# Second expert product turned round, features by tokens, and 160 instead of 128 tokens served by gathered rows

## The chip, the cores and the metric

The kernel runs on one core of a Trainium2 chip. The metric is the device time of one execution in microseconds. Engines are named as the profile names them: PE multiplies matrices (PEld is its weight load), DVE and ACT work on vectors, POOL does vector work and issues the indirect DMAs, SP issues most other DMAs.

## The reference

One encoder layer over 512 tokens of 1,024 features: two sequence mixers side by side (a state-space scan and a chunked scan), merged, then a layer of 16,384 experts, of which each token uses 128 (8 heads, 16 each), and a last norm. All is 32-bit. Only the expert layer is touched by the change:

```python
expert = (i1 * PEER_NKEYS + i2).reshape(t, PEER_HEADS * PEER_TOPK)     # 128 of 16384 for each token
gates = jax.nn.softmax(best_s, axis=-1).reshape(t, PEER_HEADS * PEER_TOPK)
...
hid = jnp.einsum('td,tkd->tk', xb, u_tab[eb])
act = jax.nn.gelu(hid, approximate=False) * gb
return jnp.einsum('tk,tkd->td', act, v_tab[eb])
```

## The kernel before

The four tiles of 128 tokens are served in two ways.

Tile 0 is **gathered** (`gathered`, L1082): for each of its 128 picks an indirect DMA on POOL fetches one row of the table per token (`rowg`, 512 KB, four buffers, three fetched ahead), 128 times from `u` and 128 times from `v`. DVE multiplies a row of `u` with the token and sums it (L1103), and adds a row of `v`, scaled, to `acc0` (L1113).

Tiles 1 to 3 are **dense** (`dense`, L1027): all 16,384 experts for all 384 tokens, in 128 blocks of 128 experts. For a block `up` (L1034) loads a tile of the transposed `u` (`w_raw`, 512 KB), splits it into a high and a low part (`wload` L137: ACT casts to `w_hi` at L143, POOL or DVE subtracts to `w_lo` at L144), and runs 24 matmuls (`mm3`, L151 to L153: 8 feature blocks, three products of parts) into `hid` [128 experts, 384 tokens]; ACT applies gelu into `F`. The second product then loads the block's rows of `v` (`v_raw`, 512 KB, three buffers of its own), splits them (`vh`, `vl`, L156 and L157), multiplies `F` with the gates (L1062), splits that (`Wh`, `Wl`), and runs 18 matmuls (L1074 to L1076) with 128 tokens as the stationary side and 512 features as the moving side, into six accumulators [128 tokens, 512 features] that stay in PSUM for all blocks.

`w_raw` has three buffers, `w_hi` and `w_lo` two each. All loads of `w_raw`, `v_raw` and the gates `G8` (1.5 MB for 8 blocks, two buffers) stand in SP's one queue, in a fixed order, each waiting for its buffer.

The gates come from `route_pick` (L921, DVE) and `gates` (L976): for each tile of tokens eight steps of 16 tokens, in which DVE, ACT and POOL build one-hot matrices, PE multiplies them (L1020), ACT copies the result (L1021) and SP stores it to DRAM (`G_d`, L1024). The first 34 `up` (NF = 34) run ahead of the dense loop and fill PE during this stage. `G8` is read back from `G_d` once all of it is stored. At the end `finish` (L1117) adds, norms and stores the four tiles.

A scheduler sets each engine's fixed order from the program's order and its own estimates; each engine then takes its list in order. The dense loop with the gathered steps between its blocks is this:

```python
for i, _ in enumerate(self.dense()):
    owed += GATHER if i < 128 - NF else (256.0 - GATHER * (128 - NF)) / (NF - 4)
    while owed >= 1.0:
        next(gathered, None)
        owed -= 1.0
```

## Time and profile before

| | |
|---|---|
| three runs | 1957.99, 1961.28, 1967.22 us (median 1961.28) |
| span of the profiled execution | 1962.9 us (no time of its own is given beside the span) |
| front and merge | to about 592 us |
| routing scores | 592 to 755 us |
| picks and gates, with `up` as filling | 755 to 1004 us |
| rest of the 34 `up` | 1004 to 1028 us |
| dense loop with both products | 1028 to 1814 us |
| dense loop, second product alone | 1814 to 1954 us |
| final norm and stores | 1954 to 1963 us |

The profiled execution lies between the middle and the slowest of the three runs, 1.6 us above the median. In the slices of the page each digit is the busy share of a fortieth of the span (49 us) in tenths.

### The profile page before, as it was taken

How to read it: one execution, taken by the hardware profiler on the slowest of the kernel's cores; microseconds unless marked ns; L12 is line 12 of the kernel's file. 1: busy time of each engine (PE TensorE's matmuls, PEld its weight loads, DVE VectorE, ACT ScalarE, POOL GpSimd, SP SyncE). 2: the span in 40 equal slices, each digit the busy share in tenths (PEclk: the TensorE clock that was granted, in tenths of full speed). 3: DMA queues.
4: the chain of work that ended last, by engine and by line, in shares of the span. 5: the costliest groups of instructions: out<-in, count | busy, mean ns of one | idle time of the engine just before them, and what ended most of it. 6: DMA issues, size and time to landing. Idle time of an engine off the chain costs nothing.

```text
span 1962.9 us, 27293 instructions
## 1 busy us (share of the span) xinstructions
PE 1817.9 (93%) x9447; PEld 1580.4 (81%) x9447; DVE 1498.9 (76%) x3238; ACT 836.4 (43%) x1426; POOL 774.4 (39%) x637
## 2 busy tenths in 40 slices
PE   6778889999998987887899999999999999999998
PEld 4666667767887877877898999999999999999886
DVE  7999875677645789998867977777777777777676
ACT  4333545455332333967762333333333333333333
POOL 3364403444112345554543543343434343343341
PEclk9889899999999998998999999999999999999999
DMA  4212153454552223424379998889899889886665
GB/s 141 91 44 82 54 139 125 157 155 141 199 180 79 98 80 129 183 108 183 119 250 334 363 334 294 305 309 313 278 314 313 301 283 313 306 284 230 234 259 200
DMA packets 174826, 407.45 MB, mean 208 GB/s; under 512 B 20000, under 2 KB 77088, under 8 KB 171616
## 3 DMA queue, kind: packets, MB, share of 16 engines
q1 hardware_dynamic: 129472, 258.27, 39.0%
q0 software_dynamic: 36864, 134.23, 19.3%
q10 hardware_dynamic: 8352, 13.21, 1.9%
q8 instruction: 74, 1.21, 0.3%
q14 instruction: 64, 0.52, 0.1%
HBM read 367.28 MB, written 37.32 MB: 206 GB/s over the span
## 4 chain that ended last, share of the span: by engine, by line
PE 59%; DVE 10%; ACT 2%; DMA 2%; issue 1%; POOL 1%; DVEq 0%; POOLq 0%; ACTq 0%
PE acc L1075 9%; PE acc L1076 9%; PE acc L1074 8%; PE hid L153 7%; PE hid L151 7%; PE hid L152 7%; PE mm L151 3%; PE mm L153 3%; PE mm L152 3%; PE sm L1020 2%; DVE oh L1001 2%; DMA G<-G_d 2%; DVE oh L1002 1%; DVE ohm L935 1%; ACT stg L1021 1%
## 5 line engine op out<-in xcount | busy, mean ns | idle before, releaser
L143 ACT CAST w_hi<-w_raw 128x1024 fp32r<-128x1024 f32 (+2 forms) x209 | 211.8, 1014 | 459.7 <-PE hid L152 220.4
L153 PE MATMUL hid<-x2h,w_lo 128*128 128x384 f32 x1024 | 357.3, 349 | 12.8 <-POOL w_lo L144 9.2
L151 PE MATMUL hid<-x2h,w_hi 128*128 128x384 f32 x1024 | 355.5, 347 | 9.7 <-ACT w_hi L143 9.7
L144 POOL TENSOR_TENSOR w_lo<-w_raw,w_hi 128x1024 fp32r<-128x1024 f32 (+1 forms) x94 | 218.6, 2327 | 361.5 <-ACT w_hi L143 354.7
L152 PE MATMUL hid<-x2l,w_hi 128*128 128x384 f32 x1024 | 355.0, 347 | 0.0
L1091 POOL DMA_INDIRECT rowg<-in_u_dram,idx x128 | 191.8, 1498 | 276.8 <-DVE rowg L1103 191.9
L1076 PE MATMUL acc<-vh,Wl 128*128 128x512 f32 x768 | 300.7, 392 | 0.0
L1075 PE MATMUL acc<-vl,Wh 128*128 128x512 f32 x768 | 300.6, 391 | 0.0
L1074 PE MATMUL acc<-vh,Wh 128*128 128x512 f32 x768 | 298.5, 389 | 0.0
L1091 POOL DMA_INDIRECT rowg<-in_v_dram,idx x128 | 167.6, 1310 | 272.2 <-DVE acc L1113 209.1
L144 DVE TENSOR_TENSOR w_lo<-w_raw,w_hi 128x1024 fp32r<-128x1024 f32 (+1 forms) x115 | 140.9, 1225 | 169.1 <-ACT w_hi L143 169.1
L153 PEld LDWEIGHTS hid<-x2h,w_lo 128*128 128x128 f32 x1024 | 197.6, 193 | 14.8 <-POOL w_lo L144 11.0
L151 PEld LDWEIGHTS hid<-x2h,w_hi 128*128 128x128 f32 x1024 | 197.4, 193 | 14.2 <-ACT w_hi L143 10.5
L156 ACT CAST Wh<-F 128x384 fp32r<-128x384 f32 x128 | 65.9, 515 | 317.8 <-PE acc L1075 279.7
L152 PEld LDWEIGHTS hid<-x2l,w_hi 128*128 128x128 f32 x1024 | 197.3, 193 | 3.7
L1076 PEld LDWEIGHTS acc<-vh,Wl 128*128 128x128 f32 x768 | 144.1, 188 | 30.3
L157 DVE TENSOR_TENSOR vl<-v_raw,vh 128x1024 fp32r<-128x1024 f32 x128 | 156.2, 1220 | 14.2 <-ACT vh L156 13.3
L1075 PEld LDWEIGHTS acc<-vl,Wh 128*128 128x128 f32 x768 | 144.1, 188 | 28.5 <-DVE vl L157 0.2
L1074 PEld LDWEIGHTS acc<-vh,Wh 128*128 128x128 f32 x768 | 144.2, 188 | 28.3 <-ACT vh L156 0.4
L1113 DVE SCALAR_TENSOR_TENSOR acc<-rowg,act,acc 128x1024 f32<-128x1024 f32 x127 | 162.4, 1279 | 5.9 <-DMA rowg<-in_v_dram,idx 5.7
L1103 DVE SCALAR_TENSOR_TENSOR rowg<-rowg,xn 128x1024 f32<-128x1024 f32 x128 | 152.0, 1219 | 5.1 <-DMA rowg<-in_u_dram,idx 5.1
L153 PE MATMUL mm<-xh,w_lo 128*128 128x512 f32 (+1 forms) x328 | 136.8, 418 | 15.9 <-DVE w_lo L144 12.3
(392 smaller groups left out, 3553.1 us busy)
## 6 DMA issues: line engine op xcount, KB each, us to landing
w_raw<-in_ut_dram SPq DMA_DIRECT2D x128, 512.0 KB, 4.7
v_raw<-in_v_dram SPq DMA_DIRECT2D x128, 512.0 KB, 6.5
G_d<-stg SPq DMA_DIRECT2D x24, 1024.0 KB, 3.9
G<-G_d SPq DMA_DIRECT2D x16, 1536.0 KB, 13.8
w_raw<-in_w_in_dram SPq DMA_DIRECT2D x40, 512.0 KB, 3.6
RB<-rows_d SPq DMA_DIRECT2D x32, 256.0 KB, 5.6
w_raw<-in_w_q_dram SPq DMA_DIRECT2D x16, 512.0 KB, 3.5
E<-rows_d SPq DMA_DIRECT2D x32, 128.0 KB, 5.0
```

The lines of the kernel that those rows point to most:

```text
L143: nc.scalar.copy(hi, raw)
L144: (lo_eng or nc.vector).tensor_sub(lo, raw, hi.bitcast(F32))
L151: mm(ps, ahi(k), bhi(k), start=start and k == 0, stop=False)
L152: mm(ps, ahi(k), blo(k), start=False, stop=False)
L153: mm(ps, alo(k), bhi(k), start=False, stop=stop and k == nk - 1)
L157: (lo_eng or self.nc.vector).tensor_sub(lo, src, hi.bitcast(F32))
L1074: mm(a, wh[:, ts], vh[:, hs], start=k == 0, stop=False)
L1075: mm(a, wh[:, ts], vl[:, hs], start=False, stop=False)
L1076: mm(a, wl[:, ts], vh[:, hs], start=False, stop=k == 127)
L1091: nc.gpsimd.indirect_dma_start(out=r, out_offset=None, in_=tab, in_offset=bass.IndirectOffsetOnAxis(ap=self.idx0[:, k:k + 1], axis=0))
L1103: d = V.scalar_tensor_tensor(r, r, 1.0, self.xn0, op0=OP.mult, op1=OP.mult, accum_out=hid[:, k:k + 1])
L1113: d = V.scalar_tensor_tensor(self.acc0, r, act[:, k:k + 1], self.acc0, op0=OP.mult, op1=OP.add)
```

## The change

- **Second product**: the host hands over `v` a second time, cut as `vt[a, d]` = 8 blocks of 128 experts (a group, `a` of 16) by 128 features (`d` of 8). `down(a, d)` loads one such tile through `wload`, so through the same `w_raw`, `w_hi` and `w_lo` buffers as `up`, and runs 24 matmuls with the features as the stationary side and the tokens as the moving side. Four of the eight feature blocks stay in PSUM, the other four are added to `yT` in SBUF by DVE after each group. `Wh` and `Wl` get 12 buffers each, since a group needs eight at once.
- **Tokens**: the dense part takes the last 352 tokens (ND). The first 32 tokens of tile 1 (NX) are gathered too: 32 tokens by 4 quarters of their picks fill 128 partitions, so 32 more rows of `u` and 32 of `v` (320 gathers in place of 256). `gates` leaves out the first two steps of tile 1.
- **Pace**: NF is 28 and GATHER 2.9. The end works in five groups of rows, with transposes of `yT` for the dense ones.

```diff
-NF = 34
+NF = 28
+NX = 32
+ND = 384 - NX
-GATHER = 2.4
+GATHER = 2.9
-LAST = 2
...
     def gates(self, t):
-        slow(0)
-        for tb in range(8):
+        first = NX // 16 if t == 1 else 0
+        slow(2 * first)
+        for tb in range(first, 8):
...
     def dense(self):
-            ps = self.phid.tile([128, 384], F32, name="hid", bufs=2)
+            ps = self.phid.tile([128, 512], F32, name="hid", bufs=2)[:, :ND]
...
-            v = vp.tile([128, 1024], F32, name="v_raw", bufs=3)
-            nc.sync.dma_start(v, I["v"][i * 128:(i + 1) * 128, :])
...
-            vh = vp.tile([128, 1024], F32R, name="vh", bufs=2)
-            vl = vp.tile([128, 1024], F32R, name="vl", bufs=2)
-            self.split(vh, vl, v)
...
-            wh = vp.tile([128, 384], F32R, name="Wh", bufs=2)
-            wl = vp.tile([128, 384], F32R, name="Wl", bufs=2)
...
-                        for hf in range(2):
-                            hs = slice(hf * 512, (hf + 1) * 512)
-                            a = self.acc[2 * t + hf]
-                            mm(a, wh[:, ts], vh[:, hs], start=k == 0, stop=False)
-                            mm(a, wh[:, ts], vl[:, hs], start=False, stop=False)
-                            mm(a, wl[:, ts], vh[:, hs], start=False, stop=k == 127)
+        def weigh(i):
+            f = F.pop(i)
+            V.tensor_mul(f, f, g8[i // 8].rearrange("p b (i t) -> p b i t", t=16)[:, :, i % 8, :])
+            w = [vp.tile([128, ND], F32R, name=n, bufs=12) for n in ("Wh", "Wl")]
+            self.split(*w, f.rearrange("p b t -> p (b t)"))
+            W[i] = w
+
+        def down(a, d):
+            hi, lo = self.wload(I["vt"][a, d], 8, 128)
+            ps = held[d] if d < 4 else pacc.tile([128, 512], F32, name="dn", bufs=2)[:, :ND]
+            one = d >= 4
+            for b in range(8):
+                wh, wl = W[8 * a + b]
+                mm(ps, hi[:, b, :], wh, start=b == 0 and (one or a == 0), stop=False)
+                mm(ps, hi[:, b, :], wl, start=False, stop=False)
+                mm(ps, lo[:, b, :], wh, start=False, stop=b == 7 and (one or a == 15))
+            if a == 15 and not one or a == 0 and one:
+                A.copy(self.yT[:, d, :], ps)
+            elif one:
+                V.tensor_add(self.yT[:, d, :], self.yT[:, d, :], ps)
+
+        gate(0)
+        for b in range(8):
+            weigh(b)
+        for a in range(16):
+            if a < 15:
+                gate(a + 1)
+            for d in range(8):
+                down(a, d)
+                if NF + 8 * a + d < 128:
+                    up(NF + 8 * a + d)
+                if a < 15:
+                    for b in range(d - 4, d - 3) if d < 7 else range(3, 8):
+                        if b >= 0:
+                            weigh(8 * a + 8 + b)
+                yield
```

How the scheduler places this, at three places that the prediction speaks of. Line numbers in the rows of the change are the changed kernel's (L1082 to L1084 are `down`, L152 to L154 `mm3`, L141 the load in `wload`, L1067 the load of `G8`, L145 its subtraction to `w_lo`).

SP's queue of before, from the last stores of the gates to the second load of `G8` (printed as `G_` with a number):

```order
L140 DMA w_raw<-in_ut_dram 128x1024
L1053 DMA v_raw<-in_v_dram 128x1024
L140 DMA w_raw<-in_ut_dram 128x1024
L1056 DMA G_10273<-G_d 128x24x128
L140 DMA w_raw<-in_ut_dram 128x1024
L1053 DMA v_raw<-in_v_dram 128x1024
L140 DMA w_raw<-in_ut_dram 128x1024
L1053 DMA v_raw<-in_v_dram 128x1024
L140 DMA w_raw<-in_ut_dram 128x1024
L1053 DMA v_raw<-in_v_dram 128x1024 x2
L140 DMA w_raw<-in_ut_dram 128x1024
L1056 DMA G_10836<-G_d 128x24x128
```

The same place of the change:

```order
L1035 DMA G_d<-stg 128x2048
L141 DMA w_raw<-in_vt_dram 128x1024
L1067 DMA G_9892<-G_d 128x22x128
L1067 DMA G_9934<-G_d 128x22x128
L141 DMA w_raw<-in_ut_dram 128x1024
L1067 DMA G_10573<-G_d 128x22x128
L141 DMA w_raw<-in_vt_dram 128x1024
L141 DMA w_raw<-in_ut_dram 128x1024
L141 DMA w_raw<-in_vt_dram 128x1024
L141 DMA w_raw<-in_ut_dram 128x1024
L1067 DMA G_11196<-G_d 128x22x128
```

Three loads of `G8` now stand ahead of the third tile of `vt`, and every tile of either product takes one of the three `w_raw` buffers.

PE of before, where the first second product begins (it stands behind 816 matmuls into `hid`, 34 `up`):

```order
L151 MATMUL hid<-x2h,w_hi 128x384
L152 MATMUL hid<-x2l,w_hi 128x384
L153 MATMUL hid<-x2h,w_lo 128x384
L1074 MATMUL acc_10265<-vh,Wh 128x512
L1075 MATMUL acc_10265<-vl,Wh 128x512
L1076 MATMUL acc_10265<-vh,Wl 128x512
L1074 MATMUL acc_10266<-vh,Wh 128x512
```

PE of the change at the same place, behind 696 matmuls into `hid` (29 `up`):

```order
L153 MATMUL hid<-x2l,w_hi 128x352
L154 MATMUL hid<-x2h,w_lo 128x352
L1082 MATMUL acc_9887<-Wh,w_hi 128x352
L1082 MATMUL acc_9888<-Wh,w_hi 128x352
L1083 MATMUL acc_9887<-Wl,w_hi 128x352
L1084 MATMUL acc_9887<-Wh,w_lo 128x352
```

In both lists the last one-hot product of the gates stands behind 668 and 667 matmuls into `hid`: between it and the first second product lay 148 of them, and now 29.

PE of the change at the border of the sixth and the seventh group (numbers tell the buffers apart: `w_hi_13632` is a tile of `up`, `w_hi_13701` the next group's first of `down`, `w_hi_13731` the `up` after it):

```order
L154 MATMUL hid_13636<-x2h_5170,w_lo_13633 128x352
L1082 MATMUL acc0_9887<-Wh_13427,w_hi_13701 128x352 [waits Activation_49]
L1083 MATMUL acc0_9887<-Wl_13428,w_hi_13701 128x352
L152 MATMUL hid_13735<-x2h_5170,w_hi_13731 128x352 [waits Activation_49]
L153 MATMUL hid_13735<-x2l_5171,w_hi_13731 128x352
L1084 MATMUL acc0_9887<-Wh_13427,w_lo_13702 128x352 [waits DVE_49]
```

Here two matmuls of the next `up` stand ahead of the third matmul of `down`; it is so at 5 of the 12 borders at which `up` still runs beside `down`, and at the others the 24 matmuls of a tile stand together.

## Rows read from the trace of the kernel before

**Rows 1.** Page: the span, and the rate of the DMAs in 40 slices.
```profile
span 1962.9 us, 27293 instructions
...
GB/s 141 91 44 82 54 139 125 157 155 141 199 180 79 98 80 129 183 108 183 119 250 334 363 334 294 305 309 313 278 314 313 301 283 313 306 284 230 234 259 200
```

**Rows 2.** Windows: stretch, its length, busy us (count) of each engine, PEclk, DMA share, GB/s.
```profile
755.00:1004.00 249.00, 206.89 (x1287) 197.16 (x1286) 229.15 (x802) 184.66 (x345) 137.99 (x121) 0.90 0.40 151
1080.00:1814.00 734.00, 734.00 (x3714) 668.38 (x3714) 551.39 (x689) 257.19 (x360) 292.99 (x216) 1.00 0.88 303
1814.00:1954.00 140.00, 139.97 (x619) 115.55 (x617) 95.59 (x123) 51.69 (x78) 44.01 (x28) 1.00 0.64 233
...
1100.00:1140.00 40.00, 40.00 (x202) 36.11 (x201) 35.78 (x39) 14.67 (x20) 17.06 (x14) 1.00 1.04 388
```

**Rows 3.** Timeline of PE: start, us. The first and last of 15, then of 24.
```profile
1499.99 0.39 PE L1074 MATMUL acc<-vh,Wh 128*128 128x512 f32 x1
...
1503.41 0.33 PE L151 MATMUL hid<-x2h,w_hi 128*128 128x384 f32 x1
...
1507.60 0.39 PE L1074 MATMUL acc<-vh,Wh 128*128 128x512 f32 x1
```

**Rows 4.** Groups by form, 1080 to 1814 us: count, busy us, mean ns, idle before, releaser.
```profile
L1113 DVE SCALAR_TENSOR_TENSOR acc<-rowg,act,acc 128x1024 f32<-128x1024 f32 x111 | 141.9, 1279 | 5.9 <-DMA rowg<-in_v_dram,idx 5.7
...
L144 DVE TENSOR_TENSOR w_lo<-w_raw,w_hi 128x1024 fp32r<-128x1024 f32 x88 | 107.8, 1225 | 166.2 <-ACT w_hi L143 166.2
...
L143 ACT CAST w_hi<-w_raw 128x1024 fp32r<-128x1024 f32 x87 | 91.5, 1051 | 232.6 <-PE hid L152 198.8 <-issue 33.0 <-DVE acc L1113 0.9
L1062 DVE TENSOR_TENSOR F<-F,G 128x384 f32<-128x384 f32 x96 | 52.6, 551 | 1.1 <-ACT F L1038 1.1
L157 DVE TENSOR_TENSOR Wl<-F,Wh 128x384 fp32r<-128x384 f32 x90 | 49.5, 550 | 3.4 <-ACT Wh L156 3.4
L156 ACT CAST Wh<-F 128x384 fp32r<-128x384 f32 x89 | 45.8, 515 | 221.8 <-PE acc L1075 189.7 <-issue 32.1
```

**Rows 5.** Timeline of all engines: a subtraction, and the next load into its buffer.
```profile
1500.40 1.23 DVE L144 TENSOR_TENSOR w_lo<-w_raw,w_hi 128x1024 fp32r<-128x1024 f32 x1 [2.59 <-ACT w_hi L143]
...
1501.65 0.33 SPq L140 DMA_DIRECT2D w_raw<-in_ut_dram  x1
```

**Rows 6.** DMA view, 1080 to 1814 us: count, KB, median us to landing.
```profile
DMA packets 90211, 222.50 MB, mean 303 GB/s; under 512 B 6433, under 2 KB 40225, under 8 KB 90163
...
w_raw<-in_ut_dram SPq DMA_DIRECT2D x85, 512.0 KB, 5.5
...
rowg<-in_v_dram,idx POOLq DMA_INDIRECT x112, 7.3
```

**Rows 7.** DMA view, 1028 to 1080 us, then 1080 to 1130 us.
```profile
G<-G_d SPq DMA_DIRECT2D x4, 1536.0 KB, 14.9
...
DMA packets 10296, 18.19 MB, mean 364 GB/s; under 512 B 486, under 2 KB 6630, under 8 KB 10293
...
w_raw<-in_ut_dram SPq DMA_DIRECT2D x7, 512.0 KB, 11.7
...
rowg<-in_v_dram,idx POOLq DMA_INDIRECT x16, 9.0
```

**Rows 8.** Timeline of SP: first and last stores of tile 1's gates, start and us.
```profile
787.66 13.68 SPq L1024 DMA_DIRECT2D G_d<-stg  x3
...
828.23 7.73 SPq L1024 DMA_DIRECT2D G_d<-stg  x2
```

**Rows 9.** DMA view, 1010 to 1028 us, and tile view of the gates' stores.
```profile
G<-G_d SPq DMA_DIRECT2D x1, 1536.0 KB, 8.4
...
DMA to landing us min/median/max: 3.8/3.9/6.7
```

**Rows 10.** Timeline at the end: the last matmul and the last product of DVE.
```profile
1953.84 0.39 PE L1076 MATMUL acc<-vh,Wl 128*128 128x512 f32 x1
...
1958.10 1.42 DVE L1133 SCALAR_TENSOR_TENSOR fo<-hfin,rsf,finw 128x512 f32<-128x512 f32 x2 [0.66 <-POOL rsf L1130]
```

More of the change, by code (lines that the diff above doesn't have):

```diff
@@ L1045, in dense @@
         vp = self.vp = c.enter_context(tc.tile_pool(name="vp", bufs=1, reuse_waits="tile"))
[L1046 to L1049 removed]
+        pacc = self.pacc = c.enter_context(tc.tile_pool(name="pacc", bufs=1, space=PSUM))
+        held = [pacc.tile([128, 512], F32, name=f"acc{i}")[:, :ND] for i in range(4)]
+        self.yT = vp.tile([128, 8, ND], F32, name="yT")
@@ new lines, in dense @@
+        gate(0)
[13 more added lines that the diff above has]
+                yield
+            for b in range(8):
+                del W[8 * a + b]
@@ L1082, in gathered, with ready @@
+    def ready(self):
+        self.xnX = self.vp.tile([128, 1024], F32, name="xnX")
+        for q in range(4):
+            self.nc.scalar.dma_start(self.xnX[32 * q:32 * q + 32], self.xq_d)
+        self.accX = self.vp.tile([128, 1024], F32, name="accX")
     def gathered(self):
@@ new lines, in finish_all @@
+    def finish_all(self):
+        nc, I = self.nc, self.I
+        T = nc.tensor
+        self.finw = self.gp.tile([128, 1024], F32, name="finw", tag="rowg", bufs=4)
+        nc.sync.dma_start(self.finw, I["rows"][1:2, :].to_broadcast([128, 1024]))
+        self.hfin = {}
+        rows = [(0, 128), (128, NX), (128 + NX, 128 - NX), (256, 128), (384, 128)]
+        for i, (t0, n) in enumerate(rows):
+            pool, tag, bufs = (self.gp, "rowg", 4) if i < 3 else (self.vp, "G8", 2)
+            h = self.hfin[t0] = pool.tile([128, 1024], F32, name="hfin", tag=tag, bufs=bufs)
+            nc.sync.dma_start(h[:n], self.h_d[t0 // 128][t0 % 128:t0 % 128 + n])
+        self.finish(0, 128, [self.acc0[:, 0:512], self.acc0[:, 512:1024]])
+        sel = self.cp.tile([128, NX], F32, name="sel")
+        nc.vector.tensor_add(sel, self.ident[:, 0:32], self.ident[:, 32:64])
+        for q in (2, 3):
+            nc.vector.tensor_add(sel, sel, self.ident[:, 32 * q:32 * q + 32])
+        ps = []
+        for hf in range(2):
+            p = self.phid.tile([128, 512], F32, name="hid", bufs=2)
+            T.matmul(p[:NX], sel, self.accX[:, 512 * hf:512 * hf + 512], start=True, stop=True)
+            ps.append(p[:NX])
+        self.finish(128, NX, ps)
+        for t0, n in rows[2:]:
+            ps = []
+            for hf in range(2):
+                pool, nm = (self.phid, "hid") if hf else (self.pacc, "dn")
+                p = pool.tile([128, 512], F32, name=nm, bufs=2)
+                for d in range(4):
+                    T.transpose(p[:n, d * 128:(d + 1) * 128],
+                                self.yT[:, 4 * hf + d, t0 - 512 + ND:t0 - 512 + ND + n], self.ident)
+                ps.append(p[:n])
+            self.finish(t0, n, ps)
@@ L1212, in whole @@
                     pass
-                self.finw = self.gp.tile([128, 1024], F32, name="finw", tag="rowg", bufs=4)
-                nc.sync.dma_start(self.finw, I["rows"][1:2, :].to_broadcast([128, 1024]))
-                self.hfin = {}
-                for t in range(4):
-                    pool, tag, bufs = (self.vp, "v_raw", 3) if t else (self.gp, "rowg", 4)
-                    self.hfin[t] = pool.tile([128, 1024], F32, name="hfin", tag=tag, bufs=bufs)
-                    nc.sync.dma_start(self.hfin[t], self.h_d[t])
-                self.finish(0, [self.acc0[:, 0:512], self.acc0[:, 512:1024]])
-                for t in range(3):
-                    self.finish(t + 1, self.acc[2 * t:2 * t + 2])
+                self.finish_all()
 def host(inputs):
```

103 lines of the change are left out of this document (55 added, 48 removed).

## The prediction

> **What bounds the kernel now.** I read the page first, for where the DMAs are busy [rows 1], then windows cut at the stages. From 1080 to 1814 us PE is busy for all 734.00 us and from 1814 to 1954 us for 139.97 of 140.00; in the same windows DVE has 551.39 and 95.59 us [rows 2]. PE's busy time overlaps itself, so I took the pace from the timeline of PE: 15 matmuls over 512 columns go by in 3.42 us (0.228 us each), 24 over 384 columns in 4.19 us (0.1746 each) [rows 3], back to back. That is 4.10 us for a second product and 4.19 us for an `up`. The dense loop is bound by PE, at the full granted clock (1.00, the 2.4 GHz level) [rows 2].
>
> The groups by form show why nothing else shows through there: DVE waits 166.2 us for ACT's cast before its subtractions, and ACT's cast waits 198.8 us for PE to give a `w_hi` back [rows 4]. Everything stands ready ahead of PE. A load goes out 0.02 us after the subtraction that frees its buffer [rows 5], and three buffers turn over once per 3 x 8.29 = 24.9 us, of which landing (5.5 us, median), cast (1.05) and subtraction (1.23) need 7.8 [rows 4, 6]. Seventeen microseconds are slack.
>
> The stage of the gates, 755 to 1004 us, is another matter: DVE 229.15, PE 206.89, ACT 184.66 of 249 us [rows 2]. Its eight stores per tile start 6.85 us apart: the first at 787.66, the last at 828.23 + 7.73 - 0.32 = 835.64, seven steps [rows 8].
>
> **The change, part by part.**
>
> *Gates.* Two of 24 steps go: -2 x 6.85 = -13.7 us. The picks of DVE between them stay. At the end of the stage as many matmuls of `up` have gone out as before (667 against 668), so the filling does not grow. Bounds: 0, if the stage ran on the filling alone, and -13.7.
>
> *From the last gate to the first second product.* Before, 148 matmuls of `up` fill it (1004 to 1028 us by the table, 24). Now 29 do, 5 us, and then PE waits for the gates' way through DRAM: the last store lands after 3.9 us, the first `G8` after 8.4 [rows 9], product, cast and subtraction of the first block take 0.55, 0.5 (a guess from the product of the same size) and 0.55 [rows 4]: 13.9 us in all, -10.1. The bound above takes 14.9 us for `G8`, as it was in the stretch with four of them [rows 7]: -3.6.
>
> *PE in the dense loop.* From the two lengths, 128 columns cost 0.0534 us, 0.417 ns a column; 352 columns make 0.1746 - 32 x 0.000417 = 0.1613 us. Bounds: 0.1600 (in proportion) and 0.1746 (no gain under 384). The first second product stands behind 696 matmuls of `up`, so 128 x 24 - 696 = 2376 of these and 128 x 24 = 3072 of `down` remain: 5448 x 0.1613 = 878.8 us, against 926 before (1028 to 1954): -47.2. A pair of `down` and `up` takes 7.74 us where it took 8.29; 24 matmuls in place of 18 are paid by shorter ones.
> The Trainium skill, in TensorE: Matmul & The Clock Gate, section Wait — 56ns, not 53.3ns?, gives columns over 2.4 GHz plus about 2.5 ns for a matmul back to back. That would be 162.5 ns for 384 columns, where the row shows 174.6, so the trace disagrees; by it 352 columns take 149.2 ns and the stretch 812.8 us, 66 less than by the rows.
>
> *DVE.* It has 551.39 us for 88 blocks, 6.27 each. New per pair: half a gather (0.5 x 1.28), an addition to `yT` for every second tile (0.5 x about 0.55, as the product with the gates, which is of the same shape), and 32 of 384 columns less on two operations (-0.09): 7.1 of 7.74 us [rows 2, 4]. Not the bound, but 92% full and in one order. After the last `up`, 95.59 us for 34 blocks is 2.8; with 0.24 gathers and the addition more, 3.4 of 3.87.
>
> *Buffers.* This is what speaks against the change. A tile of `down` now takes a `w_raw`, and no `v_raw` helps: three buffers turn over once per 3 x 3.87 = 11.6 us. Cast and subtraction need 2.3, the handoffs 0.1, so 9.2 us are left for landing and every wait on ACT and DVE. At 303 GB/s a tile lands in 5.5 us; in the stretch of 364 GB/s it took 11.7 [rows 6, 7], but with up to six tiles in flight where there are now three. The loop wants 227 tiles and 320 gathers of 0.524 MB and 16 `G8` of 1.44 MB, 310 MB in 878.8 us: 353 GB/s. For 40 us at 1100 the DMAs moved 388 with PE busy throughout [rows 2], so the rate is there; the landing is what gets tight. I take a landing near 7, between the rows and nearer to the first since half the tiles are in flight, which fits with 2 us to spare, except behind a `G8`, which goes through the same queue. There I take 1.5 us of PE's time, between nothing and the 2.5 by which 11.7 passes 9.2, for each of the 14 `G8` after the first two: +21. Bounds: 0, and 227 x (11.7 + 2.4 - 11.6) / 3 = +189, if every tile landed as in the busy stretch.
>
> *The first group.* The third `G8` waits until eight products have read the first, about 8 us of DVE, and the third tile of `vt` stands behind it in SP's queue. Landing 14.9 us, cast and subtraction 2.3: it is ready 25 us after the first `G8` landed. PE has by then the first two tiles of `down`, paced by the eight blocks (9.3 us), and an `up` (3.9): 12 us short; with 8.4 for that `G8`, 5.5 short. Gathers are running, so I take +10.
>
> *The borders.* At 5 borders of groups PE meets the next `up`, whose cast has to wait for the `up` just ended, before the third matmul of `down`: 1.1 us less the two matmuls of 0.16 that go first, 5 x 0.8 = +4; below, 0, and above, with the subtraction ahead of it on DVE, 5 x 2.0 = +10.
>
> *The end.* Before, 1962.9 - 1954.2 = 8.7 us from PE's last matmul [rows 1, 10]. Now the last addition to `yT`, transposes, and three groups of rows instead of the last one and a half follow it: I take 15, +6 (bounds +2, two more products of 1.42 less the staggered start, and +12). The extra casts, the 12 buffers of `Wh` and the stores of the 32 tokens cost nothing: ACT is busy 257.19 of 734 us [rows 2] and hides them; if it were not free, a cast in front of `w_hi` would cost its 0.5 us at each border.
>
> Sum, against the profiled 1962.9, which is 1.6 us over the median of the three runs: 1962.9 - 13.7 - 10.1 - 47.2 + 6 = 1897.9 without stalls; + 10 + 4 + 21 = **1933 us**.
>
> **The rivals.**
>
> *A: the three `w_raw` buffers set the pace; slower.* Between the sum without lateness (1912) and the time before lie 51 us, 0.225 for each of 227 tiles: from a landing with waits of 9.2 + 3 x 0.225 = 9.9 us on, the change loses. For it: on the line between 5.5 us at 303 and 11.7 at 364 GB/s, 353 GB/s gives 10.6; DVE, 92% full, adds waits in front of each subtraction. Against: three tiles fewer in flight, and a slower loop asks for less, so it settles. At 329 GB/s that line gives 8.1, with 2.1 of waiting 10.2: 4.2 us a tile, 227 x 4.2 = 953, and the time 1912 + 953 - 879 = 1986.
>
> *B: no lateness at all*: the DMAs keep 353 GB/s with landings under 9 us, as the 388 GB/s at 1100 us suggest [rows 2]. 1898 to 1912, say 1905.
>
> *C: the gathers set the pace.* Four `rowg` buffers turn over once per 4 x 7.74 / 2.9 = 10.7 us. Landing 7.3 us, in the busy stretch 9.0 [rows 6, 7], and DVE's 1.28 leave 2.1 or 0.4 for the wait on DVE and POOL. With 1 us of each, 11.3 us: a pair takes 8.19, 100 pairs +45: 1957. Against: DVE waited only 5.9 us for gathered rows of `v` in 734 [rows 4].
>
> *D: a matmul has no fixed part.* With 352 columns at 0.417 ns, 0.147 us: 5448 x 0.0143 = 78 us less, 1855. Both lengths of rows 3 speak against it. The Trainium skill's rule above would be this case nearly, at 1867.
>
> **How the numbers follow.** The forecast with some lateness, 1912 to 1951, has 0.42; A 0.25; B 0.17; C 0.14; D 0.02. About 0.5%, 10 us, is what a measurement of this kernel can tell from no change. Forecast, B and D are faster by more, 0.61; C lies within, 0.14; A is slower, 0.25. The predicted time is 1933 us. The range reaches from B's lower part to A's time, 1892 to 1988, which leaves out D, the rest of B and the half of A above it; the likeliest case alone spans 1912 to 1951.
>
> **What would show it.** Matmuls of 352 columns 0.161 us apart; the last store of the gates 14 us earlier; PE idle for some 9 us before the first `down` and again for some 10 at its third tile; in the dense loop PE waiting for DVE's `w_lo` a few microseconds per `G8` and otherwise back to back, near 345 GB/s, a landing of 7 to 8 us. The prediction is wrong if PE waits for `w_lo` or `w_hi` at most tiles (A), if DVE waits for `rowg` by tens of microseconds (C), or if 352 columns take 0.175.

## The result, and the profile after

Four runs of the changed kernel took 2021.20 to 2031.56 us, median 2026.12; four of the kernel before 1957.27 to 1967.22, median 1959.63. The ratio is 1.033 (95% interval 1.0301 to 1.0359): slower by 3.3%. The forecast of 1933 us fell on the wrong side, and the time lies outside its range of 1892 to 1988 as well. Rival A, the slower one, named the right neighbourhood with 1986 and was still 40 us short.

The page of the changed kernel, for [rows 1]: the span, and the rate of the DMAs in 40 slices of 51 us.

```profile
span 2021.3 us, 28786 instructions
...
GB/s 150 76 46 85 44 161 159 136 164 116 229 140 81 86 130 111 141 194 116 227 325 302 334 329 293 309 329 331 331 308 292 313 320 299 345 289 332 267 273 146
```

Windows of the changed kernel, for [rows 2]: both products, the second product alone, then a stretch inside the first (length, busy us and count of PE, PEld, DVE, ACT and POOL, granted clock of PE, DMA share, GB/s).

```profile
1003.00:1883.00 880.00, 807.20 (x4778) 785.73 (x4779) 697.65 (x919) 288.26 (x419) 404.75 (x289) 0.97 0.89 314
1883.00:2000.00 117.00, 111.01 (x673) 108.87 (x672) 84.88 (x113) 39.28 (x57) 35.67 (x27) 0.99 0.74 255
...
1100.00:1800.00 700.00, 646.88 (x3859) 630.13 (x3858) 554.88 (x721) 229.27 (x328) 313.05 (x233) 0.98 0.90 316
```

PE was busy for all 734 us of the dense loop before; now it stands still for 53 of 700 us, and its clock is no longer 1.00 throughout. DVE is busy for 555 of 700 us, the DMAs move 316 GB/s where 345 were forecast. No engine is full. Where PE stands still, the view of its waits says (from the first `down` to the last: us in total, times, longest):

```profile
PE dn L1084 <- DVE w_lo L145: 24.5, 25, 2.3
PE hid L152 <- ACT w_hi L144: 23.4, 12, 6.2
PE hid L154 <- DVE w_lo L145: 18.2, 15, 4.3
PE acc L1082 <- ACT Wh L157: 14.7, 1, 14.7
PE acc L1084 <- DVE w_lo L145: 11.1, 10, 3.7
```

The wait of 14.7 us lies ahead of the first `down`. The others are of two kinds, and a stretch of the timelines shows each. First the tile that **lands late**. The DMA view of the changed kernel from 1185 to 1200 us (times: issues, KB, median us to landing), then the same view from 1100 to 1800:

```profile
G<-G_d SPq DMA_DIRECT2D x1, 1408.0 KB, 17.1
w_raw<-in_ut_dram SPq DMA_DIRECT2D x2, 512.0 KB, 12.9
w_raw<-in_vt_dram SPq DMA_DIRECT2D x1, 512.0 KB, 12.7
...
w_raw<-in_vt_dram SPq DMA_DIRECT2D x81, 512.0 KB, 6.1
w_raw<-in_ut_dram SPq DMA_DIRECT2D x80, 512.0 KB, 6.6
G<-G_d SPq DMA_DIRECT2D x10, 1408.0 KB, 15.4
```

A load of the gates goes out at 1185.09 and takes 17.1 us; the three tiles issued behind it take 15.6, 12.7 and 10.2, where 6.1 to 6.6 is usual. All tiles of the stretch whose landing keeps PE waiting stand behind such a load. PE's timeline at the tile issued at 1189.17 (start, us, what, and in brackets the idle time before it):

```profile
1202.64 0.32 PE L1084 MATMUL dn<-Wh,w_lo 128*128 128x352 f32 x1
1205.99 0.66 PE L152 MATMUL hid<-x2h,w_hi 128*128 128x352 f32 x1 [3.03 <-ACT w_hi L144]
...
1207.71 0.49 PE L152 MATMUL hid<-x2h,w_hi 128*128 128x352 f32 x1
1208.00 0.49 PE L153 MATMUL hid<-x2l,w_hi 128*128 128x352 f32 x1
...
1212.87 0.32 PE L152 MATMUL hid<-x2h,w_hi 128*128 128x352 f32 x1
1213.03 0.32 PE L153 MATMUL hid<-x2l,w_hi 128*128 128x352 f32 x1
```

Behind the wait the matmuls are 0.293 us apart, up to 1212.7, and then 0.160 again. The windows show what that is: from 1208.00 to 1212.40 PE works without a pause at a granted clock of 0.50, the 1.2 GHz level. It is the same after the long wait ahead of the first `down`.

```profile
1208.00:1212.40 4.40, 4.40 (x16) 4.40 (x16) 1.29 (x2) 0.47 (x1) 0.00 (x0) 0.50 0.75 222
...
1003.42:1007.84 4.42, 4.42 (x14) 4.12 (x15) 4.42 (x11) 2.59 (x6) 0.00 (x0) 0.50 0.66 203
```

Second, the **subtraction that is late on DVE**, though its tile landed long ago. DVE's timeline, and behind it PE's:

```profile
1339.61 1.23 DVE L1143 SCALAR_TENSOR_TENSOR rowg<-rowg,xn 128x1024 f32<-128x1024 f32 x1 [1.78 <-DMA rowg<-in_u_dram,idx]
1340.76 0.08 DVE L1143 DVE_READ_ACCUMULATOR rowg<-rowg,xn 128x1 f32 x1
1340.76 0.52 DVE L1088 TENSOR_TENSOR yT<-yT,dn 128x352 f32<-128x352 f32 x1
1341.19 0.52 DVE L1071 TENSOR_TENSOR F<-F,G 128x352 f32<-128x352 f32 x1
1341.63 1.22 DVE L145 TENSOR_TENSOR w_lo<-w_raw,w_hi 128x1024 fp32r<-128x1024 f32 x1
...
1342.90 0.43 PE L1084 MATMUL dn<-Wh,w_lo 128*128 128x352 f32 x1 [0.94 <-DVE w_lo L145]
```

DVE stands still for 1.78 us until a gathered row has landed, since its order is fixed; the subtraction for PE stands three instructions further on and is ready 0.94 us too late. Over the 700 us DVE waits 38 and 23 us for rows, where the kernel before waited 4.5 and 3.9:

```profile
DVE rowg L1143 <- DMA rowg<-in_u_dram,idx: 37.9, 33, 3.3
DVE acc L1153 <- DMA rowg<-in_v_dram,idx: 22.9, 23, 2.0
```

The same view of the kernel before:

```profile
DVE rowg L1103 <- DMA rowg<-in_u_dram,idx: 4.5, 7, 1.5
DVE acc L1113 <- DMA rowg<-in_v_dram,idx: 3.9, 5, 0.9
```

For an account of the whole stretch I took the starts of its 5448 matmuls, which are all in the trace, from 1003.4 to 1999.7 us. Their usual distance is 0.160 us, which makes 872 us. What goes beyond that at a single matmul is a wait; it is put to DVE where the subtraction of its tile began over 0.3 us after the cast had ended, else to the tile's landing. What the matmuls at the lower clock took beyond 0.160 is the clock's. That gives 871.7 + 30.5 (tiles late) + 67.9 (subtractions late) + 23.5 (lower clock) + 2.8 (distances too small to be a wait) = 996 us, and the same account is used for every experiment. It measures where a wait shows, not what first caused it.

### The profile page after: what moved, and what is told of

It reads as the page before. It is cut to its first block, busy times and chain, and to the rows that moved or that the text cites. A ratio compares the mean times of both kernels' runs of the same rounds, so it can differ in the third digit from the quotient of the medians.

```text
span 2021.3 us, 28786 instructions
## 1 busy us (share of the span) xinstructions
PE 1782.5 (88%) x10179; PEld 1610.2 (80%) x10179; DVE 1585.7 (78%) x3364; ACT 819.4 (41%) x1417; POOL 847.3 (42%) x688
## 4 chain that ended last, share of the span: by engine, by line
PE 17%; DMA 15%; issue 13%; DVE 12%; POOL 6%; ACT 3%; POOLq 0%; DVEq 0%; ACTq 0%; SPq 0%
POOL rowg L1129 6%; DMA rowg<-in_v_dram,idx 5%; DMA w_raw<-in_ut_dram 3%; DMA rowg<-in_u_dram,idx 2%; PE hid L154 2%; PE hid L152 2%; PE hid L153 2%; DVE w_lo L145 2%; ACT stg L1032 2%; PE sm L1031 1%; PE acc L1084 1%; DMA rowg<-in_v_dram,idxX 1%; DVE oh L1011 1%; PE acc L1082 1%; PE acc L1083 1%
## 5 line engine op out<-in xcount | busy, mean ns | idle before, releaser
L144 ACT CAST w_hi<-w_raw 128x1024 fp32r<-128x1024 f32 (+1 forms) x337 | 346.2, 1027 | 844.7 <-PE hid L153 258.7
L145 DVE TENSOR_TENSOR w_lo<-w_raw,w_hi 128x1024 fp32r<-128x1024 f32 x249 | 304.3, 1224 | 105.1 <-ACT w_hi L144 82.8
L152 PE MATMUL hid<-x2h,w_hi 128*128 128x352 f32 x1024 | 350.0, 342 | 37.0 <-ACT w_hi L144 34.0
L154 PE MATMUL hid<-x2h,w_lo 128*128 128x352 f32 x1024 | 351.4, 343 | 28.3 <-DVE w_lo L145 18.9
L153 PE MATMUL hid<-x2l,w_hi 128*128 128x352 f32 x1024 | 349.4, 341 | 0.0
L145 POOL TENSOR_TENSOR w_lo<-w_raw,w_hi 128x1024 fp32r<-128x1024 f32 (+1 forms) x88 | 205.2, 2333 | 342.1 <-ACT w_hi L144 341.9
L152 PEld LDWEIGHTS hid<-x2h,w_hi 128*128 128x128 f32 x1024 | 204.1, 199 | 41.9 <-ACT w_hi L144 38.7
L154 PEld LDWEIGHTS hid<-x2h,w_lo 128*128 128x128 f32 x1024 | 204.2, 199 | 37.5 <-DVE w_lo L145 25.7
L1084 PE MATMUL dn<-Wh,w_lo 128*128 128x352 f32 x512 | 169.4, 331 | 24.5 <-DVE w_lo L145 24.5
L1082 PE MATMUL acc<-Wh,w_hi 128*128 128x352 f32 x512 | 166.9, 327 | 15.4 <-ACT Wh L157 14.7
L1084 PE MATMUL acc<-Wh,w_lo 128*128 128x352 f32 x512 | 168.0, 329 | 11.4 <-DVE w_lo L145 11.1
L1082 PE MATMUL dn<-Wh,w_hi 128*128 128x352 f32 x512 | 166.5, 325 | 0.0
L1083 PE MATMUL dn<-Wl,w_hi 128*128 128x352 f32 x512 | 165.8, 324 | 0.0
L154 PE MATMUL mm<-xh,w_lo 128*128 128x512 f32 (+1 forms) x328 | 135.5, 414 | 18.6 <-DVE w_lo L145 12.0
L152 PE MATMUL mm<-xh,w_hi 128*128 128x512 f32 (+1 forms) x328 | 136.6, 416 | 3.0 <-ACT ost L726 1.0
```

Of the source, the lines that this page charges most:

```text
L144: nc.scalar.copy(hi, raw)
L145: (lo_eng or nc.vector).tensor_sub(lo, raw, hi.bitcast(F32))
L152: mm(ps, ahi(k), bhi(k), start=start and k == 0, stop=False)
L153: mm(ps, ahi(k), blo(k), start=False, stop=False)
L154: mm(ps, alo(k), bhi(k), start=False, stop=stop and k == nk - 1)
L1082: mm(ps, hi[:, b, :], wh, start=b == 0 and (one or a == 0), stop=False)
```

## The experiments

All stand against the kernel before (medians 1959 to 1966 us in the several series). Three versions (e1, e2, e3) leave out work and ran once; their time has no interval. The columns of the table are us: the time, the stretch from the first to the last matmul of the second product, and the account of it.

| | time | stretch | matmuls | tiles late | DVE late | lower clock |
|---|---|---|---|---|---|---|
| changed kernel | 2026 | 996 | 872 | 31 | 68 | 23 |
| e1_no_g8 | 1986 | 952 | 872 | 3 | 65 | 12 |
| e2_no_row_dma | 1901 | 880 | 877 | 0 | 2 | 2 |
| e3_no_row_work | 2045 | 1009 | 872 | 47 | 57 | 29 |
| e4_rowg5 | 2035 | 1011 | 877 | 66 | 38 | 30 |
| e5_raw4 | 2002 | 973 | 866 | 2 | 85 | 15 |
| e6_g8_act | 2090 | 1061 | 872 | 1 | 152 | 35 |
| e7_gd | 2000 | 971 | 872 | 2 | 77 | 18 |
| q1_hl3 | 2025 | 994 | 877 | 19 | 67 | 27 |
| q2_raw4_hl3 | 1980 | 964 | 889 | 1 | 56 | 17 |
| c3_raw4_rowg5 | 2010 | 981 | 883 | 25 | 46 | 26 |
| q3_raw4_hl3_gd | 1984 | 971 | 883 | 1 | 63 | 19 |
| q4_no_gd | 1975 | 963 | 906 | 27 | 16 | 13 |
| q5_all | 1949 | 937 | 906 | 0 | 24 | 6 |
| p1_product | 2058 | 1029 | 943 | 14 | 46 | 26 |

(The column of matmuls is their number times their usual distance, 0.159 to 0.162 us at 352 columns; p1 has 384. q2 and q3 run 25 blocks of the first product ahead, q4 and q5 22, instead of 28, so 72 and 144 matmuls more stand in their stretch.)

### Which half of the change costs

**p1_product.** The turned product with all 384 tokens, and the 128 gathered ones alone; NF stays at the changed kernel's 28.

```diff
-NX = 32
+NX = 0
-GATHER = 2.9
+GATHER = 2.4
```

> The turned product alone: 384 tokens dense, 128 gathered, at 2.4 gathers an iteration. By the rows PE needs 5448 x 0.1746 = 951 us from the first to the last matmul of the second product, that starts two steps of the gates later, at 1017, and the end takes 18: 1986 us without a stall. Theory R: 278 MB in 951 us are 292 GB/s, less than either kernel moved, so stalls under 25 us, 1986 to 2010. Theory B: the tiles' way through three buffers has 12.6 us, still under the 13.1, so stalls of 40 or more, over 2025.

2058.13 us, ratio 1.0494 (1.0470 to 1.0518): worse than the whole change, though the DMAs moved only 274 GB/s and four row buffers had 8.3 us a pair for 2.4 rows, as before. Its stretch is 104 us longer than the 925 of before; 18 are matmuls, 86 waits and clock. DVE waits 66 us for rows between 1100 and 1800, where the kernel before waited 8. Its timeline shows one such wait: three rows stand one behind the other, then another. POOL had stood still for 4.76 us until the first of the three gave its buffer back, and it issued the fetch that DVE waits for here only at 1407.29.

```profile
1403.82 1.22 DVE L1139 SCALAR_TENSOR_TENSOR rowg<-rowg,xn 128x1024 f32<-128x1024 f32 x1
...
1407.25 1.22 DVE L145 TENSOR_TENSOR w_lo<-w_raw,w_hi 128x1024 fp32r<-128x1024 f32 x1
1408.39 0.55 DVE L1071 TENSOR_TENSOR F<-F,G 128x384 f32<-128x384 f32 x1
1415.96 1.22 DVE L1139 SCALAR_TENSOR_TENSOR rowg<-rowg,xn 128x1024 f32<-128x1024 f32 x1 [7.02 <-DMA rowg<-in_u_dram,idx]
1417.11 1.22 DVE L145 TENSOR_TENSOR w_lo<-w_raw,w_hi 128x1024 fp32r<-128x1024 f32 x1
```

The subtraction at 1417.11 stands behind those 7 us; PE loses 4.0 us at it.

**p2_tokens.** The other half: 352 and 160 tokens, with the second product of before in the loop (`v_raw`, `vh` and `vl` of its own, 18 matmuls over 512 columns) and 34 blocks ahead.

```diff
-NF = 28
+NF = 34
...
+            v = vp.tile([128, 1024], F32, name="v_raw", bufs=3)
+            nc.sync.dma_start(v, I["v"][i * 128:(i + 1) * 128, :])
```

> The 352 and 160 tokens alone, with the second product as before (its own three load buffers, 18 matmuls over 512 columns), 34 blocks ahead and 2.9 gathers an iteration. PE needs 94 x 24 x 0.1613 + 128 x 18 x 0.228 = 889 us, from about 1003 on, and 10 behind: 1902 us without a stall. Theory R, with the changed kernel's 317 GB/s as all that there is: 307 MB take 968 us, about 1980. Theory B: six load buffers hide the landings, stalls under 25 us, 1905 to 1930, faster than the kernel before.

1944.22 us, ratio 0.9915 (0.9894 to 0.9936): faster than before, by 0.85%, and between the two expectations. Its window from 1100 to 1800 us:

```profile
1100.00:1800.00 700.00, 698.49 (x3632) 618.14 (x3631) 581.77 (x741) 247.79 (x355) 346.93 (x254) 1.00 0.95 342
```

And the waits of DVE for rows there:

```profile
DVE rowg L1130 <- DMA rowg<-in_u_dram,idx: 44.2, 32, 3.2
DVE acc L1140 <- DMA rowg<-in_v_dram,idx: 13.9, 18, 2.4
```

The window rules out two rivals at once: the DMAs can move 342 GB/s, and DVE can be busy for 582 of 700 us, with PE full beside them. DVE waits as long for rows as in the changed kernel (58 us against 61); next to none of it reaches PE, which stands still for 1.5 of 700 us. In this version the tiles of the second product have buffers of their own; that this is why is argued, not shown, since no run gave the turned product six load buffers. What is shown is that the turned product is the whole loss, and that 32 more gathered tokens are a gain by themselves.

### What makes PE wait under the turned product

The first series set theory 1 (gates in SP's queue) against theory 2 (rows in DVE's order) and theory 3 (the DMAs' rate).

**e1_no_g8.**

```diff
         def gate(a):
+            if a >= 2:
+                g8[a] = g8[a - 2]
+                return
```

> The loads of the gates from the third on are left out (later groups use the first two again). In the changed kernel the stretch from the first to the last matmul of the second product, 996 us, is 873 us of matmuls 0.160 us apart, 31 us in which PE waits for a tile that landed late, 66 us in which it waits for a subtraction that stood in line on DVE, and 24 us of matmuls at the lower clock. Theory 1 (a load of the gates ahead of the tiles in SP's queue makes them late): the 31 us fall under 8, the clock's part by half, about 1980 us; and if a late tile is also what throws DVE back, the 66 us fall to some 35 and the time to 1945. Theory 2 (DVE waits in its fixed order for gathered rows, and the subtractions behind them are late): the 66 us stay at 55 or more, and the time is 1975 to 1990. Theory 3 (the rate of the DMAs is used up): 22 MB of 310 less, 7%, so at most 45 us and from both parts alike.

1986.24 us. Late tiles fell from 31 to 3, the clock's part by half, and the late subtractions stayed at 65: theories 1 and 2 each for its own part.

**e2_no_row_dma.**

```diff
         def fetch(tab, idx, k):
+            if len(kept) >= 4:
+                kept.append(kept[-4])
+                return kept[-1]
```

> Only the first four gathers fetch; all later products of DVE read those four rows again, so DVE's work stays and the waits for rows go, with 43% of the DMA traffic and POOL's issues. Theory 2: the 66 us of subtractions in line fall under 15, the late tiles behind a load of the gates stay at 15 to 31: 1920 to 1940 us. Theory 3: both vanish: 1900. If DVE is simply too full (it is busy 0.80 to 0.90 of the loop): the 66 us stay above 45, 1975 to 2000.

1901.28 us, as theory 3 had said (theory 2: 1920 to 1940), PE nearly without a wait:

```profile
1100.00:1800.00 700.00, 699.99 (x4338) 698.46 (x4337) 618.66 (x811) 259.92 (x373) 0.00 (x0) 1.00 0.52 159
```

DVE does all its work here, 619 of 700 us, at PE's full pace: 88% of DVE is not too much. The rows are behind both kinds of waits, by their traffic and by DVE's waiting for them; this run alone can't tell these apart. That it is no fixed rate of the DMAs near 316 GB/s, as theory 3 has it, p2 shows with 342.

**e3_no_row_work.**

```diff
-                d = V.scalar_tensor_tensor(r, r, 1.0, xn, op0=OP.mult, op1=OP.mult,
-                                           accum_out=hid[:, k:k + 1])
+                d = V.tensor_copy(hid[:, k:k + 1], r[:, 0:1])
...
-                d = V.scalar_tensor_tensor(acc, r, act[:, k:k + 1], acc, op0=OP.mult, op1=OP.add)
+                d = V.tensor_copy(acc[:, k:k + 1], r[:, 0:1])
```

> All gathers fetch as before, but DVE only copies one number out of each gathered row in place of its two products over 1024 numbers, so DVE has about 390 us less to do and the DMAs the same. Theory R (the DMAs can't land tiles and rows as fast as the loop asks, 310 MB in 879 us): PE's losses stay, now as late tiles and not as subtractions in line: 60 us or more of waits, 1970 to 2010 us. Theory V (DVE, 90% full and in a fixed order, is what is late): the 66 us of waits for subtractions fall under 10, 1930 to 1950 us.

2045.36 us, outside both expectations: DVE is busy for 340 us less (1246 against 1586), and it is not faster. DVE waits 86 + 80 us for rows between 1100 and 1800 and subtractions stay late by 57: it is the waiting in a fixed order that counts, not the work.

**e4_rowg5.** The room for the fifth buffer (4 KB of each partition) comes from `xnX`, which is read into the place of `xn0` when that is done with.

```diff
-            r = gp.tile([128, 1024], F32, name="rowg", bufs=4)
+            r = gp.tile([128, 1024], F32, name="rowg", bufs=5)
-            while len(ahead) < 3 and
+            while len(ahead) < 4 and
```

> Five buffers of gathered rows and four fetched ahead, in place of four and three (the room comes from the copy of 32 tokens, which takes the place of the 128 tokens once these are served). Theory 2: a row has 2.7 us more before DVE waits for it; DVE's 68 us of waits for rows fall under 25 and PE's 66 us for subtractions to 35 or less; with the clock 1975 to 1990 us. Theories 1 and 3: within 10 us of the changed kernel, 2015 to 2035.

2035.38 us (ratio 1.0373, 1.0326 to 1.0421). As theory 2 said, DVE's waits for rows fell (61 to 38 us in the window, though not under 25) and the late subtractions halved (68 to 38); against it, the late tiles doubled (31 to 66). It looks as if with one more row in flight the tiles' three buffers no longer do.

**e6_g8_act.**

```diff
-            nc.sync.dma_start(g8[a], ...)
+            d = (nc.scalar if a > 1 else nc.sync).dma_start(g8[a], ...)
+            if a > 1:
+                tc.keep_in_program_order(d)
...
                 down(a, d)
+                if d == 1 and 0 < a < 15:
+                    gate(a + 1)
```

> The loads of the gates from the third on go out on ACT's queue, after the second tile of a group, when their buffer has long been free, in place of SP's queue. Theory 1: no tile stands behind them, PE's 31 us for late tiles fall under 10, the clock's 24 to 15, and 1980 to 1990 us come out, less if DVE is thrown back less. Theory 3: the same bytes at the same rate, no change beyond 10 us. Theory 2: the 66 us stay.

2089.91 us, the slowest. Late tiles did fall to 1, but now the gates themselves come late; DVE waits for nine of them:

```profile
DVE F L1073 <- DMA G<-G_d: 66.3, 9, 9.5
```

It was my placing that failed: the load went out two tiles into the group, and the nine products that waited for it went on only 18 to 22 us behind its issue. Whether ACT's queue or the pieces of 512 bytes made it that slow was not tried. It says nothing against theory 1.

**e7_gd.** The gates are stored so that a group is one run of 11 KB for each partition; the runs of 512 bytes move to the stores, in the stage before.

```diff
-            self.G_d = self.dr.tile([ND // 16, 128, 128, 16], F32, name="G_d")
+            self.G_d = self.dr.tile([128, 16, ND // 16, 128], F32, name="G_d")
...
-            nc.sync.dma_start(g8[a], self.G_d.rearrange("b p i t -> p b (i t)")[:, :, a * 128:a * 128 + 128])
+            nc.sync.dma_start(g8[a], self.G_d[:, a])
```

> The changed kernel with the gates laid out in DRAM by groups: a partition reads 11 KB in one run in place of 22 runs of 512 bytes, and the stores write the runs of 512 bytes instead. If it is the small pieces that hold up the tiles behind a load of the gates: its landing falls from 15 to about 8 us, PE's 31 us for late tiles under 15, the clock's part by a third, 1990 to 2005 us. If it is the bytes: within 10 us of the changed kernel. The last store of the gates may land 2 to 4 us later.

1999.57 us (ratio 1.0198, 1.0158 to 1.0239), late tiles 31 to 2, and the gates themselves land in 10.0 us (median) instead of 15.4: the same bytes in long runs hold nobody up. It was the pieces. The late subtractions did not follow, 77.

**e5_raw4.** The second series set theory B (too few load buffers) against theory R (the DMAs' rate) and theory V (DVE too full).

```diff
+        if self.nw >= 0 and self.nw % 4 >= 3:
+            raw = self.vp.tile([128, k, m], F32, name="v_raw", bufs=1)
+        else:
+            raw = self.wp.tile([128, k, m], F32, name="w_raw", tag="w_raw", bufs=3)
```

> Every fourth tile of the dense part gets a load buffer of its own, so four turn over in place of three (the room is that of the copy of 32 tokens). Theory B (three load buffers are too few: a tile has 11.6 us for its way and needs 13.1): 15.5 us are there, PE's 31 us for late tiles fall under 10, the subtractions' 66 under 45, 1950 to 1985 us. Theory R: more tiles in flight make each land later, within 10 us of the changed kernel. Theory V: the 66 us stay, 1985 to 2000.

2002.22 us (ratio 1.0210, 1.0174 to 1.0246): one load buffer more takes the late tiles from 31 to 2, as the long runs did. The subtractions did not follow, 85, so theory B held for the tiles alone.

**q1_hl3, q2_raw4_hl3.** Three `w_hi` and `w_lo`, first alone, then with four load buffers.

```diff
+        if more and self.nw % 3 >= 2:
+            hi = self.vp.tile([128, k, m], F32R, name="v_hi", bufs=1)
+            lo = self.vp.tile([128, k, m], F32R, name="v_lo", bufs=1)
```

> Three w_hi and three w_lo for the tiles of the dense part in place of two, the load buffers still three (room: the copy of 32 tokens as before, and 11 instead of 12 buffers of Wh and Wl). Theory H (the two w_hi and w_lo that both products now share are what is short: a cast starts when PE has ended the tile before the last, and cast 1.05 and subtraction 1.22 must be done within one tile's 3.87 us, so 1.6 us of waiting on DVE shows on PE; before there were 12.4 us less 2.3): PE's 66 us for subtractions fall under 20, tiles leave their load buffers sooner, and the time is 1950 to 1980 us. Theory B (load buffers alone): within 15 us of the changed kernel, 2010 to 2035.

> Four load buffers and three w_hi and w_lo, with 25 instead of 28 blocks of the first product ahead (12 us more for PE behind the gates; the room comes from there). Theories H and B together: nearly no waits left on PE, 873 + 12 + 10 us from the first to the last matmul of the second product, 1003 before and 21 behind: 1910 to 1945 us. If the rate of the DMAs is the limit after all: over 1980.

q1 gave 2024.92 us (1.0297 to 1.0361 of before): theory H fell, the 68 us stayed at 67. q2 gave 1980.18 (ratio 1.0092), late tiles 1, subtractions still 56.

**c3_raw4_rowg5, q5_all, q3_raw4_hl3_gd, q4_no_gd.** Four load buffers and five row buffers; then everything (four `w_raw`, three `w_hi` and `w_lo`, five `rowg`, gates in long runs, NF = 22 for the room); then that without the fifth row buffer (NF = 25), and without the long runs.

> Four load buffers for tiles and five for gathered rows (11 instead of 12 buffers of Wh and Wl). Alone, the fourth load buffer took PE's waits for late tiles from 30 to 2 us and left 85 of subtractions late behind rows on DVE; the fifth row buffer alone took these from 68 to 38 and raised the late tiles to 66. Theory K (two rings of buffers coupled by DVE's fixed order: a late tile holds up the rows and a late row the tiles, and each ring needs its own slack): both go, late tiles under 10 and subtractions under 40, 1950 to 1980 us. Theory R (one rate for both, what one ring gains the other loses): sum of the waits 85 or more, 1995 to 2010.

> Everything together: four load buffers, three w_hi and w_lo, five row buffers, the gates in long runs, with 22 instead of 28 blocks ahead to make room. Theory K: waits of PE under 30 us, 1915 to 1945, level with or under the version with the tokens alone (1944). Theory R: 345 GB/s is what the version with the tokens alone moved, so 310 MB and the six blocks more need 920 us: not under 1950.

> The version with everything (1949 us) without the fifth row buffer, and with 25 blocks ahead as in the version with four load buffers and three w_hi and w_lo (1980). If the rows' own ring is what made the rest of the subtractions late: they stay near 50 us, 1965 to 1980. If the gates' long runs did it: 30 us or less, 1940 to 1955.

> The version with everything, but the gates read in runs of 512 bytes again. If the rows' own ring did it: 30 us or less of waits, 1945 to 1960. If the gates' long runs did it: the 15 us and more of a landing behind a load of the gates come back through the fuller rings, 1970 to 1990.

c3 came to 2010.04 us, the fifth row buffer bringing the late tiles back (2 to 25): about the time that theory R had said, but a sum of waits of 71, under R's 85 and over what K allowed. q5 came to 1948.61 (ratio 0.9928, 0.9898 to 0.9957), at 342 GB/s, so c3's 319 GB/s are no fixed rate: the rings need slack at once, and more of it than c3 gives. A limit of the DMAs near the 342 to 345 that p2 and q5 moved, as theory R had it for q5 ("not under 1950"), is not ruled out by these runs. The last two take q5 apart. Without the fifth row buffer 1984.44, without the long runs 1975.38; PE's longest waits are then of the one kind and of the other. Of q3, without the fifth row buffer:

```profile
PE dn L1096 <- DVE w_lo L156: 20.6, 12, 4.2
PE acc L1096 <- DVE w_lo L156: 11.8, 6, 3.7
```

Of q4, without the long runs:

```profile
PE hid L163 <- ACT w_hi L155: 11.4, 5, 7.9
PE hid L165 <- DVE w_lo L156: 7.4, 7, 2.2
```

The rows' ring makes the subtractions late (63 without the fifth buffer, 24 with it; 56 in q2 and 16 in q4, with the gates in small pieces), the small pieces of the gates make the tiles late (27 with them, none without).

### The end, and the fastest version

**p3_tokens_gd.** The tokens alone (p2), with the gates in long runs, by the edit of e7.

> The 352 and 160 tokens with the second product as before, and the gates laid out by groups. There PE waited 8 us in all in the dense loop, so the layout can give little: 1935 to 1950 us, by either theory of the small pieces.

1946.61 us (ratio 0.9908, 0.9883 to 0.9932), no change from p2, as expected: there nothing waits for a tile.

**p5_tokens_lnexp, p6_tokens_sqrt.** Behind PE's last matmul the changed kernel takes 21 us. POOL's last work is a power at 2011.07, ACT's last store goes out at 2013.11, and the span ends at 2021.3, 8.2 us later; before, the last store was 3.3 us from the end. In these 8.2 us the trace has nothing but the landing of that store, at 2015.17, and POOL's closing drain, from 2011.04 to 2020.54. Both runs take the power off POOL, in p2, whose end is like that of the changed kernel (last store at 1937.21, span 1945.4).

```diff
-        nc.gpsimd.tensor_tensor(rs, rs, self.mhalf[:n, 0:1], OP.pow)
+        A.activation(rs, rs, AF.Sqrt)
+        V.reciprocal(rs, rs)
```

> The version with the tokens alone, with the last norm's power on ACT (exp of minus half the logarithm) instead of POOL, whose last instruction is then a gather. POOL's final drain took 9.5 us behind its last power in that version and in the changed kernel, 4.3 in the kernel before. If the drain follows from POOL's own last work, it now runs beside the end: 5 us less, 1937 to 1942. If it waits for something that ends late anyway: no change, or 2 to 4 us more for ACT's tables.

> The version with the tokens alone, with the last norm's power as a square root on ACT and a reciprocal on DVE; one table that the loop's end needs once or twice, where the version with logarithm and exponential loaded eight tables of 1.3 us. If POOL's drain behind its last power is what the end was mis-sized by: last store to end 3 us in place of 8, about 5 us less than the 1944 of the tokens alone, 1936 to 1942. If not: no change.

p5 (logarithm and exponential on ACT) took 1954.18 us: the last store is 3.0 us from the end, but ACT loads a table before each, eight times 1.28 us in the chain. p6 took 1939.81 us (ratio 0.9907, 0.9878 to 0.9936), the lowest median of all versions that do the whole work; its last store, and from it 3.8 us to the end of the span at 1935.9 (p2: 8.2):

```profile
1932.03 0.36 ACTq L1162 DMA_DIRECT2D out_dram<-fo  x1
```

Between p2 and p6, which ran in different series, the intervals overlap, so the gain of 4 us is shown by the end of the trace and not by the ratio.

## Why the prediction was wrong

Its own sum, term by term. Ahead of the first `down` it was right in total, by two errors that cancel: the last store of the gates went out at 981.2 us, 21.7 earlier where -13.7 was said (it went out between 979 and 993 in the other versions with 28 blocks or more ahead and the same gates, so a part of it is scatter), and the way through DRAM took 22.2 us from there because the first `G8` took 15.0 us, the upper bound and not the 8.4 chosen. The first `down` came at 1003.4, forecast 1004.2. The matmuls of 352 columns stood 0.160 us apart, 0.1613 was said. By the rule of the Trainium skill that the prediction weighed (TensorE: Matmul & The Clock Gate, section Wait — 56ns, not 53.3ns?) it would have been 0.149; the trace disagrees again. PE saved what was forecast, 872 us against 879. DVE's load was right, 555 of 700 us and 6.9 us for a pair where 7.1 was said, and so was the landing, 6.1 and 6.6 where 7 was taken.

The late tiles were right in kind and nearly in size: 31 us, where the three terms for them (first group 10, borders 4, gates 21) made 35. Only the place was off: no tile was late in the first group (its longest stop, 3.3 us up to 1042.6, was a subtraction late on DVE), and all tiles that landed too late stand behind loads of the gates.

**The step that failed** is under *Buffers*: "9.2 us are left for landing and every wait on ACT and DVE", "which fits with 2 us to spare, except behind a `G8`". It compared mean durations with the turnover of one ring and priced every wait on DVE at nothing outside that; the point on *DVE* had ended at "Not the bound, but 92% full and in one order" and gave that order no price. What the runs showed in its place: DVE's subtractions come late behind gathered rows by 68 us, with DVE neither full (e2: 619 of 700 us, and PE waits 2 us in all) nor made free by less work (e3), and with DMAs that can do 342 GB/s (p2). In the kernel before DVE's waits for rows existed too, but small, 8 us, and behind 17 us of slack; p2 has them at full size, 58 us, and loses nothing, with buffers of its own for the second product. The turned product sends its tiles through those of the first, and there what is late on DVE or in SP's queue is late on PE. That the late subtractions come from the waits for rows is shown by e4 and by q5 against q3, and e2 agrees; that the shared buffers are what lets them through to PE is the likeliest reading, but more tile buffers alone did not take them away (85 in e5, 67 in q1, 56 in q2).

The second missing term is the **clock**: 23 us. Behind the longer stops, as that of 3.0 us at 1203, the matmuls run at the lower level; there are twelve stretches of 8 to 19 such matmuls, together about 150, each 0.133 us longer, which is 20 us; the rest are the distances at their edges. The forecast had 35 us of stops and no price for what follows them.

The third is the **end**, +12.6 us where +6 was taken and +12 the upper bound; 5 us of it is POOL's drain.

From 1933 the errors add up: 68 for DVE, 23 for the clock, -4 for the tiles, +6 for the end, -7 for matmuls, +3 of small distances make 2022, against a span of 2021.3.

Of the rivals, A was right that with the shared buffers the change loses; its mechanism (every tile late by a longer landing and some waiting on DVE) is not what came: landing stayed at 6.1 and 6.6 us at 316 GB/s, late tiles make 31 of the 98 us of waits, and PE has 63 waits for `w_hi` or `w_lo` in 227 tiles, so its sign, waits at most tiles, did not show. C's sign, DVE waiting for `rowg` by tens of microseconds, did: 61. C's mechanism covers the larger part and stood there as a rival of its own with the wrong price: it was thought of as a pace of rows (1957), and acts through what stands behind the rows. The argument against C, that DVE waited only 5.9 us for rows of `v` in 734, was taken from a kernel with 2.4 gathers a block and another order on DVE, and could not speak for this one: with 2.9 gathers and the second product of before DVE waits 58 us for rows (p2), with 2.4 and the turned product 66 (p1).

The fifth row buffer brings late tiles back with a fourth load buffer alone (c3, 25 us), and with the third `w_hi` and `w_lo` as well (q4, 27); with the long runs besides it does not (q5). Not settled: whether the long runs would do it without the third `w_hi` and `w_lo`. Nor is it settled why DVE meets its rows so much later in p1 than in the kernel before: that one has three rows in a line as well (from 1401.86 us) and does not wait there. The order is the scheduler's, and its estimates were not changed in any run. And no run gave the turned product six load buffers and four `w_hi` and `w_lo`, as both products have together in p2, which would show whether the sharing alone lets DVE's waits through.

## What to carry to other kernels

A change that lets two streams share buffers takes slack away, and slack is priced at the worst wait in front of the shared step, not at mean durations: list every in-order queue that the tile passes (SP's, ACT's, DVE's), and in each the slowest instruction that may stand ahead of it. A saving on the bounding engine is only real if that engine stays without stops, since behind a stop it may run slower for a while (here at half the clock behind twelve of them, 23 us in all). Test the parts of a change alone: here one half is worth -0.85% and the other costs 4.9%.
